# One chain for both directions' triangular inverses in the DeltaNet part of an encoder layer, with projections moved beside it

## The chip, the cores and the metric

The kernel runs on one core of a Trainium2 chip. The metric is the device time of one execution in microseconds. A core has five instruction streams that run side by side and meet through semaphores: TensorE (PE, matmuls; its weight loads are counted as PEld), VectorE (DVE), ScalarE (ACT), GpSimd (POOL) and SyncE (SP), which here does nothing but issue DMAs. Each stream executes its instructions in the order of the program.

## The reference, cut to what matters

Two layers of a hybrid encoder, on 512 tokens with 1024 features. Each layer normalises its input and projects it for three mixers: windowed attention (6 query heads on 2 key heads), a bidirectional gated DeltaNet (6 heads) and a bidirectional RWKV-7 (4 heads). Their outputs are concatenated, projected by one matrix and added to the residual; then comes a gated MLP.

```python
def layer(h, l):
    u = rms_norm(h, norm_mix[l])
    qa, ka, va, dn_qkv, dn_z, dn_a, dn_b, rw_in = split(u @ w_in[l])
    ya = banded_window_attention(rope(qa), rope(ka), va, sink[l])
    ys = gated_delta(dn_qkv, dn_a, dn_b) + reversed(gated_delta(reversed ...))
    yd = rms_norm(ys, dn_norm[l]) * silu(dn_z)
    yr = rwkv7(rw_in)
    h = h + concat([ya, yd, yr]) @ w_out[l]
    return h + gated_mlp(rms_norm(h, norm_ffn[l]))
```

Inside the DeltaNet, tokens go in 8 chunks of 64 per head. Each chunk needs the inverse of a unit lower triangular 64x64 matrix:

```python
lower = where(strict, (k_beta @ k.T) * decay, 0)
a_mat = lower + eye(C)
sol = triangular_solve(a_mat, rhs, lower=True, unit_diagonal=True)
```

With 6 heads, 8 chunks and two directions these are 96 matrices per layer.

## The kernel before

Features lie on the partitions and the 512 tokens along the free axis, so a tile of 128 features is 128x512. Float32 products are made in three matmuls: each operand is split in a high and a low part, and `product` (L313) issues high x high (L319), low x high (L320) and high x low (L321) for each k-tile of 128. A weight tile therefore passes three engines: SP loads `wr` (L305), ACT rounds it to `wh` (L308), POOL subtracts to give `wl` (L309). There are three buffers of each. A 128-column projection of the layer's input (`proj`) is 8 k-tiles, 24 matmuls of 512 columns, from two weight tiles of 128x512.

PSUM tiles come from four streams: "j" (2 buffers) for projections, "r" (3) for RWKV and attention, "d" (2) for DeltaNet, "o" (1). A projection's result stays in its "j" buffer until DVE has read it.

`layer` (L868) emits, in this order: RWKV preparation, its inverse and its scan over 8 chunks (`rwkv_scan`), with the attention projections handed in at steps 2 to 6 (K, V and the three query tiles q0, q1, q2); DeltaNet preparation (`dn_prep`) for two more head pairs; the RWKV output `rwkv_out`; the DeltaNet inverse; `finish_inverse`; the DeltaNet scan (`dn_scan`), with the gates z0, z1 and z2; `dn_out`; the output projection; the MLP. A scheduler then puts each engine's instructions in an order by its own reckoning, so an instruction can stand well ahead of where it is written.

The inverse of a 64x64 matrix is made of two 32x32 inverses and a product. `invert` (L378) does the 32x32 blocks by elimination: the blocks' rows lie on the 128 partitions (four groups of 32) and 32 problems lie along the free axis. A 32x32 transpose (L383 or L385) turns them so that each partition holds one whole problem of 32x32; then for j = 1 to 30 one instruction multiplies (L390) and one adds (L391), on r x j elements with r = 31 - j; then two transposes (L397, L398) bring it back. The forward direction's elimination runs on DVE, the backward one's on POOL, each with 60 instructions. What goes in are the negated diagonal blocks, copied by ACT in 24 instructions on 32 partitions (L984). `finish_inverse` (L401) then makes the product for the off-diagonal block with small matmuls (L411, L417), and ACT copies the parts into place (L413, L421, L425).

An attention block (`attn_head`, L830; there are 12 per layer, 3 query tiles x 4 token blocks) makes scores by matmul (L842), masks them and takes the maximum on DVE (L843), exponentials on ACT (L852), divides on DVE (L856), transposes on PE (L859) and multiplies by the values (L863). Five of them are written beside the inverse, seven in the DeltaNet scan. `rope` (L821) scales a projection on DVE (L823), rotates it by a matmul (L825), multiplies by the sine on DVE (L826) and by the cosine on POOL (L827) and adds on DVE (L828). `gate_proj` (L928) multiplies the projection by the normalisation on DVE (L931), makes a sigmoid on ACT (L932) and multiplies on DVE (L933). L695 and L696 in `dn_prep` scale keys and queries by their inverse norms, which a matmul (L693) and ACT (L346) make. In the scan of the DeltaNet, L773 is the matmul on the state and L778 the subtraction that follows on DVE. `split` (L249) makes a mixer output's high part on ACT (L253) and its low part on DVE (L254). The output projection takes 8 k-tiles for each of 8 output tiles j, 24 matmuls each.

Times below are of the second layer.

Of the kernel before, what the change touches and what calls it, by code (L numbers as in the profile page):

```python
# [14 lines left out]
P = 128  # L15
T = 512
# [20 lines left out]
def _const_array():  # L37
    """Everything here depends on shapes alone."""
# [19 lines left out]
    for name, v in (("eps", EPS), ("rweps", RW_EPS), ("one", 1.0), ("halfpi", math.pi / 2)):  # L58
        add(name, np.full((P, 1), v))
    add("ident", np.eye(P))  # L60
# [29 lines left out]
# per-feature parameters, as columns of 128 values  # L90
# [6 lines left out]
def _param_array(inputs):  # L97
    """[128, layer, column]: the parameters as they are, laid out by feature."""
# [15 lines left out]
def trunk(tc, t, out):  # L114
# [14 lines left out]
    # Slots of a tag are handed out in program order, so each stream of work has its own.  # L129
# [6 lines left out]
    def p4(*free, dt=F32):  # L136
        return bp.tile([P, *free], dt, tag="p4", bufs=20, name=nm("p4"))
# [12 lines left out]
    def sm(*free):  # L150
        return bp.tile([P, *free], F32, tag="sm", bufs=7, name=nm("sm"))

    def tiny(*free, tag="tiny"):
        return bp.tile([P, *free], F32, tag=tag, bufs=1 if len(free) > 1 else 3, name=nm(tag))

# [1 line left out]
    cst = cp.tile([P, _CONST.shape[1]], F32, name="cst")  # L157
    par = cp.tile([P, DEPTH, NPAR], F32, name="par")
# [31 lines left out]
    sinkb = [cp.tile([P, 6], F32, name=nm("sink")) for _ in range(DEPTH)]  # L190
# [7 lines left out]
    def derive_params():  # L198
        for l in range(DEPTH):
            pt = par[l]  # L200
            pc = lambda name, n: pt[:, at[name] : at[name] + n]
            dv = cp.tile([P, 24], F32, name=nm("dv"))
            # 0:8 centre weight of the token shift, 8:10 -k_k, 10:12 1-k_a, 12:16 -w0, 16:20 -a0
# [18 lines left out]
    cos_t = cp.tile([P, T], F32, name="cos_t")  # L222
    sin_t = cp.tile([P, T], F32, name="sin_t")
# [36 lines left out]
    class Norm:  # L260
        """Collects x tiles as they are finished: squares summed, x*g split in two parts."""
# [86 lines left out]
    def chunk_sums(dst, src, backward):  # L348
        """running sums over the tokens of each chunk"""
# [6 lines left out]
    def tok_major(st, src, evac):  # L356
        """[128 (h d), 512 tokens] -> [(h, token), chunk, d]; evac(dst slice maker, psum piece)"""
# [11 lines left out]
    def run(g):  # L369
        """the value a generator returns"""  # L370
# [7 lines left out]
    def invert(dpk, upper, E, work):  # L378
        """dpk [128, 32, 32]: strictly triangular 32x32 blocks N (row on the partition, problem, column).
        Returns (I-N)^-1 as it lies and transposed, in the same form; E does the elimination."""  # L380
# [19 lines left out]

    def finish_inverse(st, o1, o2, units, upper, sign):  # L401
        """units: (problem, matrix tile, chunk): fills tile[:, chunk, 0:64] with (I-N)^-1."""
# [52 lines left out]
        # normalised key  # L455
# [9 lines left out]
        # bonus  # L465
# [645 lines left out]
```

## Time and profile before

| | us |
|---|---|
| three timed runs | 1732.46, 1734.43, 1734.72 (median 1734.43) |
| span of the profiled execution | 1732.2 |
| RWKV scan from its third step, DeltaNet preparation, RWKV output | 1104 to 1176 |
| both 32x32 inverses | 1176 to 1222 |
| rest of the inverse | 1222 to 1247 |
| DeltaNet scan | 1247 to 1309 |
| DeltaNet output and output projection | 1309 to 1359 |

The profile is one execution on the chip. A group of instructions is given by its line in the program, engine and operation, what it writes and reads, count, busy time, the mean of one in ns, and the idle time just before them on their engine with what ended it. PEclk is the clock that was granted to TensorE in a stretch: 1.00 is 2.4 GHz, 0.50 is 1.2 GHz, and values between are a mix of the two. A matmul's own length in a timeline includes its way through the array; successive ones start closer together than they are long. The rows on which the prediction rests stand in their own section below.

### The profile page before, as it was taken

Reading aid. Unit: us, or ns where it says so; the run is one execution under the profiler, and the core shown is the slowest. Engines: PE = TensorE matmul, PEld = TensorE weight load, DVE = VectorE, ACT = ScalarE, POOL = GpSimd, SP = SyncE. Lnnn points to the kernel's source line nnn. Section 1 sums busy time; section 2 is a strip of 40 time slices with the busy share of each in tenths; the row PEclk is TensorE's granted clock in tenths of the full one; section 3 lists DMA queues with packets and bytes.
Section 4 is the critical chain, followed back from the end, with each engine's and each line's share of the span. In section 5 each row is a group of like instructions: output and inputs, shape, how many; then the busy total and the mean of one; then the engine's idle time right before and its main releaser. Section 6 shows DMA issues by size and latency. Waiting matters only on the chain. (4 is left out here: it accounts for less than half of the span.)

```text
span 1732.2 us, 29160 instructions
## 1 busy us (share of the span) xinstructions
PE 1537.9 (89%) x11500; PEld 1204.0 (70%) x11500; DVE 952.5 (55%) x1583; ACT 821.4 (47%) x1541; POOL 704.9 (41%) x632
## 2 busy tenths in 40 slices
PE   7988789359999999999998897982799999999997
PEld 4676666247678888888876676651577788888885
DVE  6478945775535555531136797578563455555001
ACT  5556453446445444443335754362744544444321
POOL 4321323431165555545543122426013655555553
PEclk9989979658999999999999998995799999999998
DMA  5311211100043333333342012220002333333332
GB/s 166 79 39 50 63 48 44 37 1 15 26 128 92 97 97 98 97 104 113 114 104 74 20 50 50 59 66 1 2 21 80 110 98 98 97 97 97 93 99 91
DMA packets 230537, 126.07 MB, mean 73 GB/s; under 512 B 23656, under 2 KB 221416, under 8 KB 230400
## 3 DMA queue, kind: packets, MB, share of 16 engines
q1 hardware_dynamic: 228624, 121.02, 25.0%
q10 hardware_dynamic: 1776, 3.20, 0.6%
q8 instruction: 90, 1.47, 0.4%
q14 instruction: 47, 0.39, 0.1%
HBM read 117.84 MB, written 6.34 MB: 72 GB/s over the span
## 5 line engine op out<-in xcount | busy, mean ns | idle before, releaser
L309 POOL TENSOR_TENSOR wl<-wr,wh 128x512 fp32r<-128x512 f32 (+1 forms) x408 | 555.9, 1365 | 760.9 <-ACT wh L308 714.5
L319 PE MATMUL ps<-hh,wh 128*128 128x512 f32 x1248 | 502.7, 403 | 21.2 <-ACT wh L308 18.6
L320 PE MATMUL ps<-hl,wh 128*128 128x512 f32 x1248 | 502.1, 402 | 0.0
L321 PE MATMUL ps<-hh,wl 128*128 128x512 f32 x1248 | 498.7, 400 | 0.4 <-POOL wl L309 0.4
L308 ACT ACTIVATE wh<-wr 128x512 fp32r<-128x512 f32 (+1 forms) x408 | 250.8, 618 | 444.5 <-PE ps L320 393.4
L319 PEld LDWEIGHTS ps<-hh,wh 128*128 128x128 f32 x1248 | 236.4, 190 | 80.2 <-ACT wh L308 19.5
L320 PEld LDWEIGHTS ps<-hl,wh 128*128 128x128 f32 x1248 | 236.3, 189 | 55.8 <-issue 3.7
L321 PEld LDWEIGHTS ps<-hh,wl 128*128 128x128 f32 x1248 | 235.8, 189 | 55.6 <-issue 3.9
L1063 DVE TENSOR_TENSOR p<-ps,p 128x512 f32<-128x512 f32 x16 | 11.1, 692 | 198.8 <-PE ps L321 198.8
L859 PE MATMUL ps<-cst,cv 128*128 128x128 f32 x120 | 24.9, 341 | 85.0 <-DVE cv L856 84.5
L320 PE MATMUL ps<-p,wh 128*128 128x512 f32 x256 | 99.6, 389 | 0.0
L319 PE MATMUL ps<-p,wh 128*128 128x512 f32 x256 | 99.6, 389 | 0.0
L321 PE MATMUL ps<-p,wl 128*128 128x512 f32 x256 | 99.6, 389 | 0.0
L1040 DVE TENSOR_TENSOR tr<-ps,rb 128x512 f32<-128x512 f32 x44 | 30.4, 692 | 100.3 <-PE ps L321 100.3
L859 PEld LDWEIGHTS ps<-cst,cv 128*128 128x128 f32 x120 | 15.7, 168 | 95.5 <-issue 67.4
L747 POOL TENSOR_TENSOR sm<-sm,gl 128x384 f32<-128x384 f32 x12 | 10.8, 903 | 129.9 <-DVE sm L776 72.8
L1043 DVE SCALAR_TENSOR_TENSOR td<-tr,par,td 128x511 f32<-128x511 f32 x44 | 39.1, 889 | 34.9 <-ACT td L1042 34.9
L1043 DVE SCALAR_TENSOR_TENSOR tr<-td,par,tr 128x511 f32<-128x511 f32 x44 | 36.5, 830 | 35.0 <-ACT tr L1042 35.0
L319 PEld LDWEIGHTS ps<-p,wh 128*128 128x128 f32 x256 | 48.1, 188 | 10.0
L321 PEld LDWEIGHTS ps<-p,wl 128*128 128x128 f32 x256 | 48.1, 188 | 9.9
L320 PEld LDWEIGHTS ps<-p,wh 128*128 128x128 f32 x256 | 48.1, 188 | 9.9
L279 POOL TENSOR_TENSOR tr<-tr,tr 128x512 f32<-128x512 f32 x32 | 42.8, 1337 | 28.0 <-issue 8.7
(292 smaller groups left out, 2597.6 us busy)
## 6 DMA issues: line engine op xcount, KB each, us to landing
wr<-ffn_w_up SPq DMA_DIRECT2D x176, 256.0 KB, 2.9
wr<-w_in SPq DMA_DIRECT2D x88, 256.0 KB, 2.8
wr<-ffn_w_down SPq DMA_DIRECT2D x80, 256.0 KB, 2.8
wr<-w_in SPq DMA_DIRECT2D x24, 128.0 KB, 2.4
p<-scr ACTq DMA_DIRECT2D x12, 256.0 KB, 3.6
wr<-w_out SPq DMA_DIRECT2D x32, 96.0 KB, 2.6
wr<-w_out SPq DMA_DIRECT2D x16, 192.0 KB, 3.0
p<-xt SPq DMA_DIRECT2D x8, 256.0 KB, 3.7
```

Source lines behind the costliest of these rows:

```text
L279: G.tensor_tensor(acc, self.acc, sq, add)
L308: S.activation(hi[:, :n, :], raw[:, :n, :], AF.Copy)
L309: G.tensor_tensor(lo[:, :n, :], raw[:, :n, :], hi[:, :n, :].bitcast(F32), sub)
L319: PE.matmul(o, wh, xh, start=k == 0, stop=False)
L320: PE.matmul(o, wh, xl, start=False, stop=False)
L321: PE.matmul(o, wl, xh, start=False, stop=k == n - 1)
L747: G.tensor_tensor(gs, state, flat(gl, step), mult)
L859: PE.transpose(pp[:, P * j : P * j + P], scs[g][:, P * j : P * j + P], ident)
L1040: V.tensor_tensor(u, o, nf.rb, mult)
L1043: V.scalar_tensor_tensor(a[:, 1:], u[:, :-1], w(0), a[:, 1:], mult, add)
L1063: V.tensor_tensor(x1[j], o, x1[j], add)
```

## The change

1. The two directions' eliminations become one chain on DVE (`invert_both`) over a persistent tile `pair_sq` of 128 x 2 x 32 x 32: 60 instructions on 2 x r x j elements (L432, L433). POOL no longer eliminates.
2. The negated diagonal blocks are made by six DVE instructions on 128x256 (`neg_diag32`, L418 and L420) in place of the 24 copies of ACT.
3. K and V stay in the RWKV scan. The query projections and the gates are written as a `fill` beside the inverse, one for every second elimination step. Behind them stand eight `rwkv_share(j)`: RWKV's two k-tiles of the output projection, 6 matmuls from a weight tile of 128x256; the result is added to the residual tile (L1039) and written to DRAM (`xr`, L1040).
4. The output projection takes 6 k-tiles instead of 8 for each j, 18 matmuls, and adds `xr` (L1093) in place of the residual.
5. Two of the twelve attention blocks are written behind the inverse and ten in the DeltaNet scan (two at each of the first three steps).
6. The pool of 128x1024 tiles has 24 buffers for 20; small constants, parameters and tables share one tile `fixed`.

By the scheduled order, q0's and z0's products still stand in the RWKV scan; q1, z1, q2, z2 and the shares stand beside the inverse. The order is the same in both programs up to the third step of the RWKV scan and from the MLP on.

```diff
+    def neg_diag32(dst, mt, upper):
+        lo, hi, m = mt[:, :, 0:32], mt[:, :, 32:64], C("m32")
+        if upper:
+            V.scalar_tensor_tensor(dst, hi, m[:, 1:2], lo, mult, sub)
+        else:
+            V.scalar_tensor_tensor(dst, lo, m[:, 0:1], hi, mult, sub)
+
+    def invert_both(dpks, work):
+        L = pair_sq
+        for d in range(2):
+            a = L[:, d]
+            V.transpose(a.rearrange("p s t -> p t s") if d else a, dpks[d].rearrange("q p t -> q t p"))
+        yield
+        for j in range(1, 31):
+            r = 31 - j
+            tmp = work[:, : 2 * r * j].rearrange("p (d r j) -> p d r j", d=2, j=j)
+            V.tensor_tensor(tmp, L[:, :, j + 1 : 32, j : j + 1].broadcast_to([P, 2, r, j]), L[:, :, j : j + 1, 0:j].broadcast_to([P, 2, r, j]), mult)
+            V.tensor_tensor(L[:, :, j + 1 : 32, 0:j], L[:, :, j + 1 : 32, 0:j], tmp, add)
+            yield
+        G.memset(L.rearrange("p d a b -> p d (a b)")[:, :, 0:1024:33], 1.0)
...
@@ layer
-            if i >= 2:
-                heads += [next(ap, None)]
-        k, vt, *qs = heads[:5]
+            if i in (2, 4):
+                heads += [next(ap)]
+        k, vt = heads
...
+        yh, yl = p4(2, T, dt=F32R), p4(2, T, dt=F32R)
+        for pr_, y in enumerate(yr):
+            S.activation(yh[:, pr_, :], y, AF.Copy)
+            V.tensor_tensor(yl[:, pr_, :], y, yh[:, pr_, :].bitcast(F32), sub)
+        rw_parts = [(yh[:, pr_, :], yl[:, pr_, :]) for pr_ in range(2)]
+        wo = t["w_out"][l]
+        wr = wo[768:1024].rearrange("(k p) m -> p k m", p=P)
+        xr = dp.tile([P, KT, T], F32, name=nm("xr"))
+
+        def rwkv_share(j):
+            xo = t2("r")
+            nc.sync.dma_start(xo, xd[:, j, :])
+            o = ps("j")
+            product(o, weights(lambda raw, k0, k1: [(raw, wr[:, k0:k1, P * j : P * j + P])], 2), rw_parts)
+            V.tensor_tensor(xo, o, xo, add)
+            nc.sync.dma_start(xr[:, j, :], xo)
+
+        def fill():
+            for i in range(3):
+                qs.append(next(ap))
+                yield
+                gate_proj(i, zss[i])
+                yield
+            for j in range(KT):
+                rwkv_share(j)
+                yield
...
             for p in range(NPAIR_DN):
-                for h in range(0, P, 32):
-                    S.activation(dpk[h : h + 32, 8 * p : 8 * p + 8, :], dn["rm"][p][d][h : h + 32, :, h % 64 : h % 64 + 32], AF.Copy, scale=-1.0)
+                neg_diag32(dpk[:, 8 * p : 8 * p + 8, :], dn["rm"][p][d][:, :, 0:64], d == 0)
             dpks.append(dpk)
-        work = cv()
-        fw, bw = invert(dpks[0], True, V, work[:, :256]), invert(dpks[1], False, G, work[:, 256:])
+        both_ways, filler = invert_both(dpks, cv()), fill()
         for i in range(31):
-            next(bw)
-            next(fw)
-            if i % 6 == 5:
-                next(att, None)
-        inv = [run(fw), run(bw)]
+            next(both_ways)
+            if i % 2 == 1:
+                next(filler, None)
+        inv = run(both_ways)
+        for _ in range(2):
+            next(att)
...
-        gate_proj(0, zss[0])
         dn["o"] = [p4(2, T), p4(2, T)]
         for i, _ in enumerate(dn_scan(dn)):
-            if i < 2:
-                gate_proj(1 + i, zss[1 + i])
             next(att, None)
+            if i < 3:
+                next(att, None)
...
-        mixed = [split(y, None, "h", i) for i, y in enumerate(yt + yr + yd)]
+        mixed = [split(y, None, "h", i) for i, y in enumerate(yt + yd)]
...
-            nc.sync.dma_start(xo, xd[:, j, :])
+            nc.sync.dma_start(xo, xr[:, j, :])
             o = ps("j")
-            product(o, weights(pieces, KT), mixed)
+            product(o, weights(pieces, 6), mixed)
```

The order on DVE at the start of the inverse, in the first layer, before. `p_2919` is the forward direction's tile, `cv_2916` the products; L843 to L856 are an attention block:

```order
L385 STREAM_TRANSPOSE p_2917<-p_2902 128x32x32
L383 STREAM_TRANSPOSE p_2919<-p_2888 128x1024
L843 ISA cv_2942,mx_2944<-ps_2945,cst,sink_86 128x256
L843 ISA mx_2944 128x1
L390 TENSOR_TENSOR cv_2916<-p_2919 128x30
L843 ISA cv_2943,mx_2944<-ps_2948,cst,sink_86 128x256
L843 ISA mx_2944 128x1
L391 TENSOR_TENSOR p_2919<-p_2919,cv_2916 128x30
L847 TENSOR_TENSOR es_2952<-sink_86,mx_2944 128x2
L848 TENSOR_SCALAR nmx_2951<-mx_2944 128x2
L390 TENSOR_TENSOR cv_2916<-p_2919 128x58
L391 TENSOR_TENSOR p_2919<-p_2919,cv_2916 128x29x2
```

The same place after. `at_` and `tr_` are the query ropes, `p_2735` is the gate z1, which DVE takes from PSUM `ps_2810`:

```order
L427 STREAM_TRANSPOSE pair_sq<-p_2749 128x32x32
L872 TENSOR_TENSOR at_2798<-at_2798,tr_2799 128x512
L432 TENSOR_TENSOR cv_2754<-pair_sq 128x60
L975 TENSOR_TENSOR p_2735<-ps_2810,rb_88 128x512
L433 TENSOR_TENSOR pair_sq<-pair_sq,cv_2754 128x2x30
L867 SCALAR_TENSOR_TENSOR tr_2897<-ps_2857,rb_88 128x512
L432 TENSOR_TENSOR cv_2754<-pair_sq 128x116
L433 TENSOR_TENSOR pair_sq<-pair_sq,cv_2754 128x2x29x2
L432 TENSOR_TENSOR cv_2754<-pair_sq 128x168
L433 TENSOR_TENSOR pair_sq<-pair_sq,cv_2754 128x2x28x3
L432 TENSOR_TENSOR cv_2754<-pair_sq 128x216
L977 TENSOR_TENSOR p_2735<-p_2735,tr_2847 128x512
```

The elimination had attention blocks between its steps; now its steps share DVE's order with the ropes (L867, L870, L872) and gates (L975, L977), and L975 and L867 read projections from PSUM.

The DMA issues on SP at the same place, before. `wr` are weight tiles, here those of the output projection:

```order
L619 DMA tr_2850<-aside_157 128x512
L620 DMA tr_2851<-aside_157 128x512
L305 DMA wr_3719<-w_in 128x4x128
L305 DMA wr_4529<-w_out 64x3x128 x2
L619 DMA tr_2868<-aside_157 128x512
L620 DMA tr_2869<-aside_157 128x512
L305 DMA wr_4529<-w_out 128x128
L305 DMA wr_4537<-w_out 128x128
```

And after. `xr_2743` is the new tile in DRAM; the weight tiles of 128x2x128 are those of the shares:

```order
L318 DMA wr_3161<-w_out 128x2x128
L1036 DMA tr_3053<-xt 128x512
L1036 DMA tr_3074<-xt 128x512
L1036 DMA tr_3095<-xt 128x512
L1036 DMA tr_3116<-xt 128x512
L1036 DMA tr_3137<-xt 128x512
L1040 DMA xr_2743<-tr_3053 128x512
L1036 DMA tr_3158<-xt 128x512
L318 DMA wr_3182<-w_out 128x2x128
L1040 DMA xr_2743<-tr_3074 128x512
L1036 DMA tr_3179<-xt 128x512
L318 DMA wr_3203<-w_out 128x2x128
```

The loads of the output projection's weights and residual have moved behind the shares' loads and, from L1040 on, between writes that each wait for a sum on DVE.

## Rows read from the trace of the kernel before

**Rows 1.** Page: span, busy time of PE, and one group of DVE.

```profile
span 1732.2 us, 29160 instructions
...
PE 1537.9 (89%) x11500; PEld 1204.0 (70%) x11500; DVE 952.5 (55%) x1583; ACT 821.4 (47%) x1541; POOL 704.9 (41%) x632
...
L1040 DVE TENSOR_TENSOR tr<-ps,rb 128x512 f32<-128x512 f32 x44 | 30.4, 692 | 100.3 <-PE ps L321 100.3
```

**Rows 2.** Windows: stretch, length, busy PE, PEld, DVE, ACT, POOL, clock, DMA share, GB/s.

```profile
1104.00:1176.00 72.00, 57.65 (x692) 39.22 (x690) 43.59 (x71) 39.10 (x84) 22.46 (x27) 0.93 0.21 60
1176.00:1222.00 46.00, 16.64 (x60) 9.73 (x60) 42.24 (x102) 8.06 (x27) 31.76 (x62) 0.54 0.00 1
1222.00:1247.00 25.00, 19.55 (x410) 14.52 (x412) 11.90 (x23) 19.94 (x51) 0.00 (x0) 0.69 0.01 2
1247.00:1309.00 62.00, 58.89 (x1074) 46.58 (x1067) 38.53 (x123) 31.65 (x87) 8.38 (x8) 1.00 0.05 15
1309.00:1361.00 52.00, 48.48 (x201) 36.80 (x199) 20.02 (x27) 26.78 (x45) 30.19 (x23) 1.00 0.39 112
```

**Rows 3.** Timeline of PE, half clock then full: start, length, line.

```profile
1084.31 0.63 PE L320 MATMUL ps<-hl,wh 128*128 128x512 f32 x1
1084.73 0.63 PE L321 MATMUL ps<-hh,wl 128*128 128x512 f32 x1
...
1329.76 0.39 PE L320 MATMUL ps<-hl,wh 128*128 128x512 f32 x1
...
1331.12 0.39 PE L320 MATMUL ps<-hl,wh 128*128 128x512 f32 x1
```

**Rows 4.** Groups by line of DVE from 1104 to 1176.

```profile
L828 DVE TENSOR_TENSOR at<-at,tr 128x512 f32<-128x512 f32 x4 | 4.0, 993 | 1.8 <-POOL tr L827 1.8
...
L826 DVE TENSOR_TENSOR at<-ps,sin_t 128x512 f32<-128x512 f32 x4 | 2.8, 688 | 1.7 <-PE ps L825 1.7
...
L593 DVE TENSOR_TENSOR sm<-ps,sm 128x256 f32<-128x256 f32 x5 | 2.1, 425 | 4.5 <-PE ps L590 4.5
L823 DVE SCALAR_TENSOR_TENSOR tr<-ps,rb 128x512 f32<-128x512 f32 x3 | 2.0, 683 | 0.0
```

**Rows 5.** Waits of DVE, 1140 to 1176: us in total, times, longest.

```profile
DVE p L385 <- ACT p L984: 8.1, 1, 8.1
DVE cv L695 <- ACT td L346: 4.2, 1, 4.2
DVE cv L696 <- ACT td L346: 2.2, 1, 2.2
```

**Rows 6.** Groups by line of ACT from 1164 to 1176.

```profile
L984 ACT ACTIVATE p<-p 32x256 f32<-32x256 f32 x24 | 9.9, 414 | 0.3
```

**Rows 7.** Groups by form of DVE from 1015 to 1068, RWKV's inverse.

```profile
L383 DVE STREAM_TRANSPOSE p<-p 128x1024 f32<-128x1024 f32 x1 | 2.0, 1958 | 0.0
...
L390 DVE TENSOR_TENSOR tr<-p 128x240 f32<-128x240 f32 x2 | 0.8, 400 | 0.0
...
L390 DVE TENSOR_TENSOR tr<-p 128x30 f32<-128x30 f32 x2 | 0.4, 198 | 0.1
```

**Rows 8.** Groups by form of DVE from 1176 to 1220, the DeltaNet inverse.

```profile
L390 DVE TENSOR_TENSOR cv<-p 128x238 f32<-128x238 f32 x2 | 1.3, 667 | 0.1
```

**Rows 9.** Timeline of DVE and POOL in RWKV's inverse.

```profile
1039.27 1.48 DVE L391 TENSOR_TENSOR p<-p,tr 128x240 f32<-128x240 f32 x1
...
1039.22 1.26 POOL L309 TENSOR_TENSOR wl<-wr,wh 128x512 fp32r<-128x512 f32 x1 [7.59 <-ACT wh L308]
```

**Rows 10.** Groups by line of DVE from 1247 to 1309, the DeltaNet scan.

```profile
L843 DVE CUSTOM_DVE_ANT_0 cv<-ps,cst,sink 128x384 f32<-128x384 f32 (+1 forms) x12 | 6.1, 548 | 0.4 <-PE ps L842 0.4
...
L856 DVE TENSOR_SCALAR cv<-cv,den 128x384 f32<-128x384 f32 (+1 forms) x14 | 4.8, 389 | 0.2
...
L778 DVE TENSOR_TENSOR sm<-ps,sm 128x384 f32<-128x384 f32 x6 | 3.3, 558 | 12.3 <-PE ps L773 12.3
```

**Rows 11.** Timeline of DVE, the last DeltaNet part's split.

```profile
1320.94 0.69 DVE L254 TENSOR_TENSOR hl<-p,hh 128x512 fp32r<-128x512 f32 x1 [0.70 <-ACT hh L253]
```

More of the change, by code (lines that the diff above doesn't have):

```diff
@@ L59, in _const_array @@
         add(name, np.full((P, 1), v))
+    hi32 = (i % 64 >= 32).astype(np.float32)
+    add("m32", np.stack([hi32 - 1.0, -hi32], 1))
     add("ident", np.eye(P))
@@ L136, in p4 @@
     def p4(*free, dt=F32):
-        return bp.tile([P, *free], dt, tag="p4", bufs=20, name=nm("p4"))
+        return bp.tile([P, *free], dt, tag="p4", bufs=24, name=nm("p4"))
     def t2(stream, *free, dt=F32):
@@ L150, in sm @@
     def sm(*free):
-        return bp.tile([P, *free], F32, tag="sm", bufs=7, name=nm("sm"))
+        n = math.prod(free)
+        a = bp.tile([P, T], F32, tag="sm", bufs=7, name=nm("sm"))[:, :n]
+        return a.rearrange("p (a b) -> p a b", b=free[1])
+    small_at = {}
     def tiny(*free, tag="tiny"):
+        if len(free) > 1:
+            lo = W + DEPTH * NPAR + 2 * T + 48 * small_at.setdefault(tag, len(small_at))
+            names = " ".join("abc"[: len(free)])
+            return fixed[:, lo : lo + math.prod(free)].rearrange(f"p ({names}) -> p {names}", **dict(zip("abc", free)))
         return bp.tile([P, *free], F32, tag=tag, bufs=1 if len(free) > 1 else 3, name=nm(tag))
-    cst = cp.tile([P, _CONST.shape[1]], F32, name="cst")
-    par = cp.tile([P, DEPTH, NPAR], F32, name="par")
+    W = _CONST.shape[1]
+    fixed = cp.tile([P, W + DEPTH * NPAR + 2 * T + 384], F32, name="fixed")
+    cst = fixed[:, :W]
+    par = fixed[:, W : W + DEPTH * NPAR].rearrange("p (l n) -> p l n", l=DEPTH)
     n0, n1 = CONSTS["ident"][0], PARAM_AT["dn_conv"]
@@ L189, in trunk @@
     cols, abias, acoef = [], [], []
-    sinkb = [cp.tile([P, 6], F32, name=nm("sink")) for _ in range(DEPTH)]
+    sinkb = [fixed[:, W + DEPTH * NPAR + 2 * T + 288 + 6 * l :][:, :6] for l in range(DEPTH)]
     def late_params():
@@ L201, in derive_params @@
             pc = lambda name, n: pt[:, at[name] : at[name] + n]
-            dv = cp.tile([P, 24], F32, name=nm("dv"))
+            dv = fixed[:, W + DEPTH * NPAR + 2 * T + 240 + 24 * l :][:, :24]
             V.tensor_tensor(dv[:, 0:8], pt[:, at["rw_mu"] : at["rw_mu"] + 8], pt[:, at["rw_mu"] + 8 : at["rw_mu"] + 16], add)
@@ L219, in trunk @@
     exp_ln_tables()
-    cos_t = cp.tile([P, T], F32, name="cos_t")
-    sin_t = cp.tile([P, T], F32, name="sin_t")
+    pair_sq = cp.tile([P, 2, 32, 32], F32, name="pair_sq")
+    cos_t, sin_t = fixed[:, W + DEPTH * NPAR : W + DEPTH * NPAR + T], fixed[:, W + DEPTH * NPAR + T : W + DEPTH * NPAR + 2 * T]
     def rotary_tables():
@@ L399, in invert @@
         return o1, o2
+    def neg_diag32(dst, mt, upper):
[17 more added lines that the diff above has]
+        G.memset(L.rearrange("p d a b -> p d (a b)")[:, :, 0:1024:33], 1.0)
+        res = []
+        for d in range(2):
+            o1, o2 = p4(32, 32), p4(32, 32)
+            nat, swp = L[:, d], L[:, d].rearrange("p a b -> p b a")
+            V.transpose(o1.rearrange("q p c -> q c p"), swp if d else nat)
+            V.transpose(o2.rearrange("q p c -> q c p"), nat if d else swp)
+            res.append((o1, o2))
+        return res
     def finish_inverse(st, o1, o2, units, upper, sign):
@@ L836, in attn_head @@
             m0 = P * (k0 - nb + 1)
-            scs = [cv(384), cv(384)]
+            scs = [cv(), cv()]
             mxt = tiny(2, tag="mx")
@@ L888, in layer @@
                 nc.sync.dma_start(wau[64:128], t["rw_a_up"][l].rearrange("d r c -> r d c"))
-                gup = bp.tile([P, 256], F32, tag="gup", name=nm("gup"))
+                gup = bp.tile([P, T], F32, tag="gup", name=nm("gup"))[:, :256]
                 nc.sync.dma_start(gup, t["rw_g_up"][l])
@@ L973, in layer @@
         yr = [rwkv_out(l, rw, pr_, None) for pr_ in range(2)]
-        pa, pb, pc_ = p4(2, T), p4(2, T), None
+        pa, pb, pc_ = p4(2, T), p4(2, T), p4(2, T)
         yt = [pa[:, 0, :], pa[:, 1, :], pb[:, 0, :]]
-        zss = [pb[:, 1, :]]
+        zss = [pb[:, 1, :], pc_[:, 0, :], pc_[:, 1, :]]
         att = attention()
+        qs = []
+        yh, yl = p4(2, T, dt=F32R), p4(2, T, dt=F32R)
[22 more added lines that the diff above has]
+                yield
         dpks = []
```

7 lines of the change are left out of this document (2 added, 5 removed).

## The prediction

> **What bounds the kernel now.** The page's head comes first [rows 1]: PE is busy for 89% of the span, so most of the 1732.2 us is matmuls in a row, and what leaves PE's list or fills a hole in it counts. The order of the two programs differs only between the third step of the RWKV scan and the end of the output projection, in layer 1 from 1104 to 1361 us. The table of stages [rows 2] is read next. From 1104 to 1176 (RWKV scan, DeltaNet preparation, RWKV output) PE is busy 57.65 of 72 us and DVE 43.59; here PE is late. From 1176 to 1222 (the inverse) DVE is busy 42.24 of 46 us, POOL 31.76, PE 16.64 at a granted clock of 0.54: DVE is the bound and PE has a hole of some 30 us. Then come ACT's stage (1222 to 1247: ACT 19.94 of 25), the DeltaNet scan (PE 58.89 of 62) and the output projection (PE 48.48 of 52). The first layer goes through the same stages, so I work in layer 1 and double.
>
> **The change part by part, per layer.** A 512-column product costs the matmuls' pitch: at full clock six of them lie between 1329.76 and 1331.12, 0.227 us each; at the half clock it is 1084.73 - 1084.31 = 0.42 [rows 3].
>
> *RWKV scan and preparation, 72.2 us.* Of 120 such products 48 stay (q0, z0); q1, q2 and z1 leave. That is 72 x 0.227 = 16.3 us less for PE, whose 57.65 falls to about 41, level with DVE. What DVE gains in time: the ropes of q1 and q2, 2 x (0.683 + 0.688 + 0.993) = 4.7 us, and about half of the waits beside them (1.8 and 1.7), 1.7 [rows 4]. DVE waits 4.2 and 2.2 us at L695 and L696 [rows 5] for a normalisation whose matmul stands behind those products on PE: 6.4, gone. Last, L385 waits 8.1 us [rows 5] for 24 ACT copies of 0.414 us (9.9) [rows 6]; six DVE instructions on 128x256 take their place. The nearest row is L593's, 128x256 with two operands, at 0.425 [rows 4]; 6 x 0.425 = 2.5 are added, and two subtractions for the share's second part, 2 x 0.69 = 1.4 [rows 11]. The scan's waits on PE, 4.5 at L593 [rows 4], fall by about another 1.0. Sum: -4.7 -1.7 -6.4 -8.1 +2.5 +1.4 -1.0 = **-18**. If L695's wait is a chain and no queue, and the scan's waits stay, it is about -10; if all of L593's go and as much again at the lines beside it, -23.
>
> *Inverse, 46.0 us.* Before, DVE has 30 pairs of instructions of r x j elements and POOL has as many; after, DVE has 30 pairs of 2rj. Without POOL beside it such an instruction took 198 ns for 30 elements and 400 for 240 [rows 7]: 169 + 0.962 per element. The sum of rj over j = 1 to 30 is 4960, so the 60 take 2 x (30 x 169 + 0.962 x 9920) = 29.2 us, with 0.035 of gap each 31.3; a 480-element one is beyond the rows and read off the line. Two transposes at 1.96 [rows 7] add 3.9. So the chain itself is 35 us: less than the 42 of before, because POOL's own elimination had made DVE's slower (667 ns for 238 elements, where 400 had done [rows 8]).
> The work beside it goes through DVE as well, and in DVE's order: three gates at 2 x 0.69 (4.1), the last of q0's rope (0.7, the size of L826), the ropes of q1 and q2 (4.7), eight sums of the shares at 0.692 (5.5, priced as L1040 [rows 1]) and the DVE side of two attention blocks, 4.7. Sum 54.7.
> POOL now splits weights here: about 5 of 128x512 and 9 of 128x256, and two rope products, some 15 us. The nearest row: an elimination instruction of 240 elements, 0.40 alone, took 1.48 beside one L309 of 1.26 on POOL, a loss of 1.08 [rows 9]. Seven long ones by 1.08 and nine short by about half would be 12; not each meets a two-input instruction from SBUF, and I take 10. Below, none, if POOL's fall into instructions that read PSUM: L1040, one operand from PSUM, kept 0.692 on the average of 44 in the feed-forward part, where POOL splits weights all along. Above, POOL's whole 15.
> DVE also waits in order on PE now: L975 (gate), L867 (rope) and L1039 (share) each stand between elimination instructions; if the product is late, the elimination behind it stands still. PE needs 144 x 0.227 = 32.7 us plus two attention blocks, well under the stage, so I count 2. Total 67: **+21**, bounds +11 and +30.
> The Trainium skill (SBUF — State Buffer, Who interferes with whom) says that a DVE instruction with two SBUF inputs contends with a GpSimd instruction that reads SBUF, and that the one that comes second is blocked for the other's whole length. The 1.08 of 1.26 agrees for one pair; applied to every POOL instruction it gives the 15 instead of the 10, which is the rival "whole hold" below.
> ACT's wh copies and sigmoids (ACT is busy 8.06 of 46) are hidden by DVE. SP's reads of x and writes of the shares stand between weight loads, and each write waits for a sum on DVE, with the loads of the next weights behind it. The loads run two or more ahead, so nothing; if that lead is gone, some 2 us a load, inside the range.
>
> *Finish of the inverse, 25 us.* Bound by ACT's small copies, of the form of those in [rows 6]; ACT is busy 19.94 of 25 [rows 2]. Its attention part moves away, transposes are now four in a row: **-3**, between -5 and 0.
>
> *DeltaNet scan, 62 us.* Ten attention blocks instead of seven, gate's work gone. A block has on DVE 2 x 0.548 and 2 x 0.389 [rows 10] plus small ones, in all some 2.4. 3 x 2.4 = 7.2, less the four gate instructions of 0.69 there (2.8), is 4.4. PE's share is hidden only in part: DVE waits 12.3 us at L778 for PE [rows 10], which says that PE's own chain sets the step, and z2's 24 products (5.4) leave it as the blocks' matmuls come. I take +4, and +1 for the last block's chain: **+5**, between +1 and +8.
>
> *Output, 49.5 us.* 48 products fewer are 10.9 us. The last DeltaNet part is split at 1320.94 [rows 11]; until then only products of the finished parts can fill PE, now 18 instead of 30 per two tiles. That gives back about 2: **-9**, between -11 and -5. Reading xr instead of x costs the same transfer.
>
> Sum: -18 + 21 - 3 + 5 - 9 = -4 a layer, -8 in all. The profiled execution's 1732.2 us lie 2.2 under the median of the runs, 1734.43; the same offset gives 1724.2 + 2.2 = **1726 us**.
>
> **The rivals.**
> *Light POOL.* The POOL holds and the waits on PE hardly bite, and the inverse is 57: -14 a layer, -28, about **1706**. For it: the chain's 35 us is simple arithmetic, and a DVE reading PSUM kept its time beside POOL. Against: half of DVE's added work has two SBUF inputs.
> *Whole hold.* Every POOL instruction costs DVE its whole length: +5, net +1 a layer, about **1736**.
> *The slower side: PE stays at the half clock in the inverse.* Its products now come in groups of 24 and 6, each after weights or an evacuation that DVE's order delays. The stage stood at 0.54 with PE busy 16.64 of 46 [rows 2], and the finish stage at 0.69 though PE was busy 19.55 of 25: being busy for most of a stage did not bring the clock up. At 0.42 instead of 0.22 the 144 products take 62 us, and with the blocks' matmuls of some 7 and the elimination waiting in DVE's order about 77 are needed: +10, net +6 a layer, about **1746**. It decides if the granted clock of this stage reads under about 0.75.
> *RWKV scan a chain.* If L695's and the scan's waits stay, that stage gives only 10: net +4 a layer, about **1742**.
>
> **How the numbers follow.** A measurement of this kernel can tell about 0.2%, 3.5 us, from no change. The forecast of 1726 has 0.42, with an own range of 1718 to 1734 (0.35 of it under 1731, 0.07 within 3.5 us); light POOL 0.22, whole hold 0.12 (0.09 within, 0.03 slower), half clock 0.16, scan a chain 0.08. Faster 0.57, same 0.16, slower 0.27. Both signs have weight, since the net is a difference of -30 and +26. The range runs from 1704, a little under light POOL, to 1745, just short of the half clock's full price; about 0.1 lies below and 0.1 above.
>
> **What would show it.** In the profile of after: the inverse stage (from the first L427 to the last L433) at 60 to 72 us with 60 elimination instructions summing to 30 us plus what POOL holds; DVE's waits on L975, L867 and L1039 summing to under 5; no wait on a copy ahead of L427; the stretch from the RWKV scan to L427 some 18 shorter; the output projection at 40 us; the granted clock of the inverse above 0.75. The forecast is wrong if the inverse lies beyond 57 to 76, if the clock stays low, or if the stretch ahead of it shrinks by under 10.

## The result, and the profile after

The changed kernel took 1740.09 us (median of 8 runs) against 1732.78 us (8 runs of the kernel before): a ratio of 1.0051, 95% interval 1.0034 to 1.0068. It is slower; 1726 was forecast, and a gain was given the larger chance. The profiled execution of after (span 1747.0 us, 14.8 above that of before) is the slowest of its eight, whose times go with the clock granted to TensorE over the whole span (1736.0 us at 0.935, 1748.8 at 0.922), so up to 4 us a layer of the growth below belong to this execution and not to the median.

Windows of the second layer after, with the columns of [rows 2]: RWKV scan and preparation, inverse, its finish, DeltaNet scan, output.

```profile
1112.50:1165.80 53.30, 42.47 (x640) 31.12 (x638) 41.32 (x74) 28.80 (x60) 17.45 (x22) 0.95 0.18 46
1165.80:1225.00 59.20, 42.74 (x149) 30.28 (x149) 56.06 (x104) 15.09 (x36) 19.05 (x17) 0.79 0.36 113
1225.00:1246.50 21.50, 16.04 (x404) 13.28 (x402) 8.70 (x10) 18.22 (x44) 0.00 (x0) 0.50 0.01 2
1246.50:1325.70 79.20, 71.77 (x1089) 54.68 (x1088) 39.73 (x147) 31.02 (x95) 5.13 (x6) 0.92 0.02 5
1325.70:1380.00 54.30, 46.74 (x168) 33.17 (x167) 23.83 (x28) 26.57 (x48) 29.35 (x25) 0.91 0.35 105
```

Cut at the same events in both kernels (from the third step of the RWKV scan; then first transpose of the inverse, first transpose back, first matmul of the DeltaNet scan, last sum of the scan, first evacuation of the MLP), the mean of the two layers is:

| stage | before, us | after, us | change | forecast |
|---|---|---|---|---|
| RWKV scan, preparation | 71.9 | 53.4 | -18.4 | -18 |
| inverse | 45.8 | 60.8 | +14.9 | +21 |
| finish | 25.9 | 21.4 | -4.5 | -3 |
| DeltaNet scan | 63.2 | 80.8 | **+17.6** | +5 |
| output | 55.8 | 53.9 | **-1.9** | -9 |

Three stages came out as worked out or better. The scan took all of it back, and the output projection gave little.

The inverse first. The two groups of the elimination, on DVE, in the second layer (line, count, busy us, mean ns, idle):

```profile
L433 DVE TENSOR_TENSOR pair_sq<-pair_sq,cv 128x60 f32<-128x60 f32 (+14 forms) x30 | 18.7, 623 | 0.5
L432 DVE TENSOR_TENSOR cv<-pair_sq 128x60 f32<-128x60 f32 (+14 forms) x30 | 17.3, 577 | 0.5
```

Together 36.0 us, where the straight line through [rows 7] gave 29.2. The largest step lies near that line when nothing holds it (480 elements: 0.658 us, 0.631 by the line). Of the other 6.8 us, 6.2 are in the 16 instructions that overlap one of POOL's; POOL is busy 19.05. So POOL costs the elimination about a third of POOL's time here, not its whole length. The waits on PE in DVE's order, of which 2 us were forecast, sum there to 2.0 us (1.0 at L1039, 1.0 at L887) and in the first layer to 3.7.

The scan is told by PE's score matmuls (L842 before, L886 after) and the last products of a block (L863, L907). In the scan before, start and length:

```profile
1273.61 0.83 PE L863 MATMUL ps<-tr,at 128*64 128x128 f32 x8
1275.44 0.70 PE L842 MATMUL ps<-at,at 64*128 64x256 f32 x4
1281.24 0.65 PE L863 MATMUL ps<-tr,at 128*64 128x128 f32 x4
1282.79 0.65 PE L863 MATMUL ps<-tr,at 128*64 128x128 f32 x4
1283.86 0.92 PE L842 MATMUL ps<-at,at 64*128 64x384 f32 x4
1289.82 1.14 PE L863 MATMUL ps<-tr,at 128*64 128x128 f32 x12
1291.73 0.92 PE L842 MATMUL ps<-at,at 64*128 64x384 f32 x4
```

And after:

```profile
1270.44 0.65 PE L907 MATMUL ps<-tr,at 128*64 128x128 f32 x4
1271.39 0.91 PE L886 MATMUL ps<-at,at 64*128 64x384 f32 x2
1272.22 0.65 PE L907 MATMUL ps<-tr,at 128*64 128x128 f32 x4
1272.81 0.91 PE L886 MATMUL ps<-at,at 64*128 64x384 f32 x2
1278.53 1.20 PE L907 MATMUL ps<-tr,at 128*64 128x128 f32 x12
1279.66 0.92 PE L886 MATMUL ps<-at,at 64*128 64x384 f32 x4
1286.85 1.19 PE L907 MATMUL ps<-tr,at 128*64 128x128 f32 x12
1287.97 0.70 PE L886 MATMUL ps<-at,at 64*128 64x256 f32 x4
```

In both, one block's scores start as the last one's product ends or soon after, 8 us apart (1283.86 to 1291.73 before, 1271.39 to 1279.66 to 1287.97 after). After, that holds for the whole scan: the scores of nine blocks start from 1254.20 to 1318.1, 8.0 us apart on average. Ten blocks at 8 us are 80, and the scan of after is 80.8. Before, one block stands in each step of the scan, its scores 0.8 to 1.3 us ahead of the step's matmuls on the state (L750), so the same rows don't tell whether the blocks or the state set the pitch there.

### The profile page after: what moved, and what is told of

It is laid out like the page before. It is cut to its first block, busy times and chain, and to the rows that moved or that the text cites. A ratio compares the mean times of both kernels' runs of the same rounds, so it can differ in the third digit from the quotient of the medians.

```text
span 1747.0 us, 29033 instructions
## 1 busy us (share of the span) xinstructions
PE 1564.1 (90%) x11500; PEld 1226.6 (70%) x11500; DVE 1021.4 (58%) x1611; ACT 786.2 (45%) x1509; POOL 653.7 (37%) x526
## 5 line engine op out<-in xcount | busy, mean ns | idle before, releaser
L332 PE MATMUL ps<-hh,wh 128*128 128x512 f32 x1216 | 491.4, 405 | 18.7 <-ACT wh L321 17.8
L333 PE MATMUL ps<-hl,wh 128*128 128x512 f32 x1216 | 491.7, 405 | 8.6 <-DVE hl L270 4.4
L334 PE MATMUL ps<-hh,wl 128*128 128x512 f32 x1216 | 484.8, 399 | 0.4 <-POOL wl L322 0.4
L332 PE MATMUL ps<-p,wh 128*128 128x512 f32 x288 | 114.0, 396 | 7.0 <-ACT wh L321 4.2
L334 PE MATMUL ps<-p,wl 128*128 128x512 f32 x288 | 113.7, 395 | 0.3 <-POOL wl L322 0.3
L333 PE MATMUL ps<-p,wh 128*128 128x512 f32 x288 | 113.5, 394 | 0.0
L332 PEld LDWEIGHTS ps<-p,wh 128*128 128x128 f32 x288 | 54.7, 190 | 20.9 <-ACT wh L321 5.4
L791 POOL TENSOR_TENSOR sm<-sm,fixed 128x384 f32<-128x384 f32 x12 | 10.3, 855 | 157.4 <-DVE sm L822 79.7
L1109 DVE TENSOR_TENSOR tr<-ps,rb 128x512 f32<-128x512 f32 x44 | 30.4, 692 | 59.4 <-PE ps L334 59.4
L333 PEld LDWEIGHTS ps<-p,wh 128*128 128x128 f32 x288 | 54.8, 190 | 11.2
L887 DVE CUSTOM_DVE_ANT_0 cv<-ps,fixed 128x256 f32<-128x256 f32 (+1 forms) x48 | 25.3, 549 | 61.3 <-PE ps L886 61.3
L1112 DVE SCALAR_TENSOR_TENSOR td<-tr,fixed,td 128x511 f32<-128x511 f32 x44 | 40.0, 909 | 36.1 <-ACT td L1111 36.1
L1113 DVE SCALAR_TENSOR_TENSOR tr<-td,fixed,tr 128x511 f32<-128x511 f32 x44 | 56.9, 1292 | 1.6
L1115 ACT ACTIVATE tr<-tr 128x512 f32<-128x512 f32 x44 | 27.8, 633 | 61.5 <-DVE tr L1113 61.4
L1112 DVE SCALAR_TENSOR_TENSOR tr<-td,fixed,tr 128x511 f32<-128x511 f32 x44 | 33.8, 768 | 35.0 <-ACT tr L1111 35.0
```

The lines of the kernel that those rows point to most:

```text
L332: PE.matmul(o, wh, xh, start=k == 0, stop=False)
L333: PE.matmul(o, wh, xl, start=False, stop=False)
L334: PE.matmul(o, wl, xh, start=False, stop=k == n - 1)
L887: V.tensor_tensor_reduce(scs[g][:, :W], pss[:, :W], C("attm")[:, m0 : m0 + W], 1.0, sinkb[l][:, tq + 3 * g : tq + 3 * g + 1], add, mx, mxt ...
L1109: V.tensor_tensor(u, o, nf.rb, mult)
L1112: V.scalar_tensor_tensor(a[:, 1:], u[:, :-1], w(0), a[:, 1:], mult, add)
```

## Experiments

Each ratio is to the kernel before, timed on the same chip. Scan and other stages are means of the two layers, cut as in the table above.

**Five blocks beside the inverse again.** The attention blocks alone are put back.

```diff
             if i % 2 == 1:
                 next(filler, None)
+            if i % 6 == 5:
+                next(att)
         inv = run(both_ways)
-        for _ in range(2):
-            next(att)
...
             next(att, None)
-            if i < 3:
-                next(att, None)
```

> The changed kernel with five attention blocks written beside the inverse and seven in the DeltaNet scan, as before; all else as changed. Theory 'blocks': each attention block in the scan costs about 3 us, because its maximum and its division stand on VectorE ahead of the state's own instructions; three fewer shorten the scan from about 80 to about 71 us in each layer and lengthen the inverse by 3 x 2.4 = 7 us; net -2 a layer, about 1736 us in all. Theory 'clock': the scan is long because TensorE enters it at the half clock; then the scan falls by under 4 us, the inverse grows by 7, and the time is about 1747 us.

Measured 1720.27 us, ratio 0.9908 (0.9889 to 0.9927). Its inverse, finish and scan in the second layer:

```profile
1148.30:1213.40 65.10, 47.91 (x197) 32.55 (x197) 59.84 (x122) 19.25 (x50) 16.91 (x16) 0.83 0.26 81
1213.40:1238.40 25.00, 17.55 (x416) 13.14 (x414) 12.39 (x23) 21.72 (x54) 1.27 (x1) 0.73 0.18 59
1238.40:1297.80 59.40, 57.39 (x1032) 46.27 (x1032) 33.20 (x116) 23.42 (x71) 5.04 (x6) 0.94 0.03 7
```

The scan falls by 21.4 us, not 9; inverse and finish together grow by 7.8. That is 7 us for each of three blocks in the scan, with what the clock does in it (0.94 here, 0.87 and 0.92 in after), and 2.6 for each outside it. The direction of "blocks" was right; its reason (a block's VectorE work ahead of the state's) gives less than half.

**The gate z2 in the finish.** Its 24 products are tied there through their PSUM stream.

```diff
-        o = proj(l, parts, COL_Z + P * pr_)
+        o = proj(l, parts, COL_Z + P * pr_, st=st)
...
+        late = (2,)
...
             finish_inverse("d", *inv[d], [(8 * p + c, dn["rm"][p][d], c) for p in range(3) for c in range(NCH)], d == 0, -1.0)
+            if d == 0:
+                for i in late:
+                    gate_proj(i, zss[i], "d")
```

> The changed kernel with the products of the gate z2 (24 matmuls) taken from the inverse and tied to the finish of the inverse, between the two directions; all else as changed. Theory 'clock': these products bring the granted clock up before the scan starts; the clock of the scan reads above 0.95 instead of 0.87 to 0.92, its first step falls by 4 us, the scan to about 75 us, finish +1, inverse -2: -5 a layer, about 1730 us. Theory 'blocks': the scan stays within 2 us of 80, and the time within 4 us of 1740.

Measured 1742.82 us, ratio 1.0041 (1.0024 to 1.0057): no difference from the changed kernel. Finish and scan of the second layer:

```profile
1218.50:1245.70 27.20, 21.19 (x431) 17.27 (x432) 10.87 (x17) 23.05 (x56) 1.97 (x2) 0.75 0.06 17
1245.70:1317.60 71.90, 63.28 (x1070) 49.18 (x1066) 38.19 (x137) 28.30 (x87) 5.65 (x6) 0.98 0.02 6
```

The clock of the scan did rise to 0.98 and the scan fell to 71.9, but one block had moved ahead of it as well, and the finish paid 6 us. The run doesn't separate the clock from the moved block, and the clock is not had for nothing.

**No shares.** The output projection takes its eight k-tiles and the residual again.

```diff
-            for j in range(KT):
-                rwkv_share(j)
-                yield
...
-            product(o, weights(pieces, 6), mixed)
+            product(o, weights(pieces, KT), mixed)
```

> The changed kernel without the shares of RWKV beside the inverse: the output projection takes its eight k-tiles and the residual again, as before. Theory 'filler': the shares took away the matmuls that filled TensorE while the DeltaNet output was made, so the output stage grows by only about 3 us when they come back, and the inverse loses 8 sums of 0.69 and the waits and POOL work beside them, about 8 us: -5 a layer, about 1730 us. Rival, as forecast: 48 products cost 9 us in the output stage and the inverse gives back 6: +3 a layer, about 1746 us.

Measured 1732.00 us, ratio 0.9976 (0.9963 to 0.9988). The output stage grows by 2.8 us for 48 products that alone take 10.9, as "filler" had it; the inverse gives back 2.0 us and not 8, the stretch ahead of it 5.5. Its scan, with the same ten blocks, is 75.4 us at a clock of 0.96, 5.4 shorter than in after (0.92 in the second layer, 0.87 in the first). Cut at the second group of matmuls on the state (L794), after's scan and then this one's are, in the second layer:

```profile
1246.50:1265.10 18.60, 16.50 (x185) 12.48 (x184) 6.35 (x22) 7.73 (x22) 1.26 (x2) 0.68 0.01 2
1265.10:1325.70 60.60, 55.27 (x906) 42.20 (x904) 33.38 (x125) 23.29 (x73) 3.87 (x5) 0.99 0.02 6
```

```profile
1231.20:1245.90 14.70, 14.05 (x185) 10.73 (x184) 6.37 (x22) 5.99 (x17) 0.84 (x1) 0.79 0.01 2
1245.90:1306.50 60.60, 54.94 (x904) 41.72 (x904) 33.37 (x125) 23.34 (x73) 4.19 (x5) 1.00 0.02 6
```

The whole difference lies in the first part, where the clocks differ (in the first layer 21.9 us at 0.53 against 14.7 at 0.79). The half clock covers 13.2 and 20.7 us of after's two scans and 6.1 of each here. Where PE sets the pace, a stretch at the half clock does half the work of one at the full clock, and half of the excess, 3.6 and 7.3 us, is close to the 3.9 and 7.2 by which the first parts differ, so the clock accounts for the 5.4; no run changes the clock alone.

**All three edits.**

> All three of these edits together: five blocks beside the inverse, z2 in the finish, no shares; one chain on VectorE, the VectorE negation and the queries and gates z0, z1 beside the inverse stay. If the three causes add up: per layer 53.5 before the inverse, 59 inverse, 22 finish, 67 scan, 57 output, 258.5 in place of 270: about 1718 us. If they do not add (the same TensorE time is only moved about), about 1730 us.

Measured 1723.28 us, ratio 0.9924 (0.9907 to 0.9941): between the two expectations. Six blocks are left in the scan, which takes 55.6, but the finish takes 35.7 us with the blocks and z2 in it.

**Five blocks, no shares.** The first and the third edit together.

> The changed kernel with five attention blocks beside the inverse (as in e1_blocks5) and without RWKV's shares (as in e3_no_share); z2 stays beside the inverse. If the share's price seen in e3_no_share (6 us a layer) is its own and not that of the clock in the scan, the time falls from the 1720 of e1_blocks5 to about 1708 us. If most of those 6 us were the scan's clock, which five blocks beside the inverse already cure, it stays at 1716 to 1722 us.

Measured 1722.13 us, ratio 0.9916 (0.9897 to 0.9935): the second case, at its upper edge. Without shares the stretch up to the inverse is 6 us shorter, but the finish goes to 29.9 us at a clock of 0.50, where it takes 25.0 at 0.73 with the shares just ahead of it:

```profile
1209.90:1239.80 29.90, 25.68 (x422) 17.86 (x422) 11.38 (x22) 21.80 (x55) 0.00 (x0) 0.50 0.01 2
```

**Eight blocks, and all twelve, ahead of the scan.** One block at every fourth step of the elimination, or at every second.

```diff
+            if i >= 4 and i % 4 == 0 and done < 8:
+                next(att)
+                done += 1
```

> The changed kernel with eight attention blocks written beside the inverse and four in the scan; shares stay. Theory 'five us a block in the scan, two to two and a half outside it', read from scans of 55.6, 59.4, 71.9 and 75.4 us with 6, 7, 9 and 10 blocks: three fewer than in e1_blocks5 take the scan from 59.4 to about 46 us and add 7 before it: -6 to -8 a layer, about 1706 us. Rival 'the state's chain is the floor': a step without a block still takes 6.5 us, the scan stays above 52, and the time is about 1722 us.

> The changed kernel with all twelve attention blocks written ahead of the finish of the inverse; the scheduler may still let a few slip into the first steps of the scan. A measure of the scan's steps without a block. By 5 us a block the later steps take about 4.5 us each and the scan about 45; the ten blocks cost some 22 us ahead of it, so the time is about 1722 us. By the rival a step without a block takes 6.5 us, the scan stays above 52 and the time goes to 1736 us or more.

Measured 1731.05 us (0.9977, 0.9961 to 0.9993) and 1736.38 us (0.9996, 0.9977 to 1.0014). The scan of the first falls only to 55.7, that of the second to 53.0. Three blocks still end in the first steps of the second one's scan; the steps behind them, without a block, take 5.2 to 5.7 us, not 6.5 and not 4.5. From e1_blocks5 to e6_blocks8 the rest of the layer grows by 9.2 us for three blocks, some 3 each. My 5 us a block was a straight line through points of a curve with a bend: with three, four and six blocks the scan takes 53.0, 55.7 and 55.6 us, with seven 59.4, and with ten 75.4 to 80.8. That below the bend the state's own chain sets the length fits these runs.

**The negation alone, in the kernel before.** `neg_diag32` in place of the 24 copies.

> The kernel before with one part of the change alone: the negated diagonal blocks by six VectorE instructions in place of ScalarE's 24 copies. VectorE's wait of 8.1 us ahead of the inverse goes and 2.5 us of work come: -5.6 a layer, -11 us in all. Rival: the wait only changes its name (another engine is as late there), and the time stays within 3 us of the kernel before.

Measured 1723.67 us, ratio 0.9929 (0.9910 to 0.9948). The stretch up to the inverse falls by 5.9 us a layer. This one part is worth 12 us, most of what any variant here gained: the 0.9908 of e1_blocks5 can't be told from it, the 0.9890 of e13_best just can.

**One block a step.** Two are left over and are written behind the scan.

```diff
             next(att, None)
-            if i < 3:
-                next(att, None)
```

> The changed kernel with the same two attention blocks ahead of the scan, but only one written at each of its eight steps; the two that are left are written behind the scan. Theory 'backlog': a block that is written steps ahead of where it runs stands in front of the state's own instructions on VectorE and TensorE, and makes a step 9.5 to 10.5 us with one or one and a half blocks in it, where a block that lags makes it 7.4; with one a step the scan's middle steps fall to about 7.5, the two blocks behind cost about 6, and scan and output together fall by about 12 us a layer: about 1718 us. Theory 'count': ten blocks cost what ten cost, wherever written; the time stays within 5 us of 1740.

Measured 1745.51 us, ratio 1.0066 (1.0040 to 1.0092). The scan falls to 62.3, and the output stage grows from 53.9 to 73.1. PE there, behind the scan:

```profile
1312.02 0.92 PE L886 MATMUL ps<-at,at 64*128 64x384 f32 x4
1312.86 1.12 PE L856 MATMUL ps<-td,fixed 128*128 128x512 f32 x2
1319.29 1.54 PE L903 MATMUL ps<-fixed,cv 128*128 128x128 f32 x6 [5.31 <-DVE cv L900]
1320.77 2.18 PE L907 MATMUL ps<-tr,at 128*64 128x128 f32 x12
1322.88 1.23 PE L886 MATMUL ps<-at,at 64*128 64x256 f32 x4
1327.44 1.08 PE L903 MATMUL ps<-fixed,cv 128*128 128x128 f32 x4 [3.33 <-DVE cv L900]
```

"Backlog" falls as an account of the whole: the three blocks that end behind the scan cost 19 us there, 6 each, with PE waiting for DVE inside (5.31 and 3.33 us in the rows). So a block in a chain is dear behind the scan too; beside the inverse it cost 2.6 us (e1_blocks5).

**Four blocks.** Beside the inverse, and one a step.

> The changed kernel with four attention blocks beside the inverse and one at each of the eight steps of the scan. By the prices so far (a lagging block about 2 us in the scan, 3 ahead of it) it is 0 to 1 us a layer shorter than e1_blocks5: about 1719 us. If a block in the scan costs 5 us whatever its place, it is 2 us a layer longer: about 1725 us.

Measured 1723.05 us, ratio 0.9938 (0.9914 to 0.9961). It doesn't tell the two apart.

**Seven blocks, written early.** The blocks of the first experiment, with two at each of the first three steps.

> e1_blocks5 with one edit: its seven blocks in the scan are written two at each of the first three steps and one at the fourth, so they run ahead of the steps; the number in the scan is the same. Theory 'backlog': the first four or five steps take 9.5 to 11 us in place of 6.1 to 8.9, the last ones 5.5; the scan grows from 59.4 to 66 or more, +6 a layer, about 1733 us. Theory 'count': the scan stays within 2 us of 59.4 and the time within 4 us of 1720.

Measured 1730.68 us, ratio 0.9987 (0.9971 to 1.0004). The scan takes 64.3 against 59.4: with the blocks done early the last steps run bare. The place counts for 5 us; the other 16 to after's scan are the number and the clock together.

**More room in PSUM.** By now the chain of blocks was seen. Each block needs four PSUM tiles of stream "r", of whose three slots one is held by the output of the whole head. The edit gives the transposes the two slots of "j", idle in the scan.

```diff
+    pp_stream = ["r"]
...
-                pp = ps("r")
+                pp = ps(pp_stream[0])
...
+        pp_stream[0] = "j"
         for i, _ in enumerate(dn_scan(dn)):
```

> The changed kernel with one edit: the attention blocks in the scan put their transposes into the two PSUM slots of stream j, which is idle there, in place of the two free slots of stream r. Theory 'chain of blocks, made by PSUM': the next block's scores no longer wait for the last one's product, the pitch of the blocks falls from 8 us to 6.5 or less while there is a backlog, the scan from about 80 to about 67, the time to about 1716 us. Theory 'the blocks' own work': PE and VectorE have no room for a second block in a step; the pitch stays at 7.5 or more, the scan above 75 and the time above 1732 us.

Measured **1717.98 us, ratio 0.9894 (0.9878 to 0.9910)**. Nothing else of the change was touched, and ten blocks still end in the scan, though three of them, not one, now have their scores in the finish, which grows by 2.1 us. Its scan, and PE in it (scores are L888, products L909):

```profile
1226.80:1292.50 65.70, 62.39 (x1074) 50.01 (x1074) 39.17 (x139) 29.21 (x92) 5.04 (x6) 0.94 0.02 6
```

```profile
1248.54 1.15 PE L909 MATMUL ps<-tr,at 128*64 128x128 f32 x12
1250.46 0.91 PE L888 MATMUL ps<-at,at 64*128 64x384 f32 x4
1251.79 0.70 PE L888 MATMUL ps<-at,at 64*128 64x256 f32 x2
1255.16 0.88 PE L905 MATMUL ps<-fixed,cv 128*128 128x128 f32 x6
1256.35 1.20 PE L909 MATMUL ps<-tr,at 128*64 128x128 f32 x12
1257.48 0.66 PE L905 MATMUL ps<-fixed,cv 128*128 128x128 f32 x4
1258.44 0.87 PE L909 MATMUL ps<-tr,at 128*64 128x128 f32 x8
1260.09 0.70 PE L888 MATMUL ps<-at,at 64*128 64x256 f32 x4
1267.16 0.92 PE L888 MATMUL ps<-at,at 64*128 64x384 f32 x4
1275.02 0.92 PE L888 MATMUL ps<-at,at 64*128 64x384 f32 x4
1282.94 0.70 PE L888 MATMUL ps<-at,at 64*128 64x256 f32 x4
```

At 1251.79 the next block's scores run while the block before still waits for its transposes (1255.16), and the two blocks' last products end within 1.8 us of each other (1257.55 and 1259.31). The scan falls from 80.8 to 65.1, and from e3_no_share's 75.4, at about the same clock, by 10.3. So the chain that kept the backlog of blocks from overlapping was made by the two free slots. From 1260.09 on, with the backlog gone and one block in each step, the blocks still follow each other at 7.1 to 7.9 us: that pitch is not the slots'.

The Trainium skill (Perfetto Trace Analysis, Optimization Strategy) says that a gap that repeats on an engine that should be full can mean that SBUF or PSUM has no room for the next tile. The sign doesn't show here: in after PE has no idle stretch above 0.72 us between 1260 and 1320, and what repeats is the blocks' pitch of 8 us. The cause does: the run with two slots more shows that PSUM was short.

**Both.** That edit on the kernel with five blocks beside the inverse.

> e1_blocks5 (five blocks beside the inverse, seven in the scan, one a step) with the transposes of the scan's blocks in stream j. Seven blocks at 8 us are 56 of its scan of 59.4, so by 'chain of blocks, made by PSUM' the scan falls to the 55 seen with four to six blocks, about -4 a layer, and the time to about 1712 us. By the rival it stays within 4 us of 1720 us.

Measured 1717.05 us, ratio 0.9890 (0.9874 to 0.9905): the shortest of all, by less than can be told from e12_more_psum, and within the 4 us of the rival. The scan falls from 59.4 to 57.9, not to 55:

```profile
1234.90:1292.90 58.00, 56.17 (x1023) 45.92 (x1022) 32.80 (x109) 22.94 (x71) 5.03 (x6) 0.92 0.03 7
```

With seven blocks, one a step, the slots are worth 1.6 us of the scan. That their chain filled the scan of seven blocks isn't borne out.

## Why the prediction failed

**The scan (+5 forecast, +17.6) is the step that failed.** It priced a block at its DVE busy time, "in all some 2.4" us, and took three of them less the gates' work. A block is scores on PE, maximum on DVE, exponentials on ACT, division on DVE, transposes on PE, copy on ACT, product on PE, one after another; its length was 8 us, and the next could not begin ahead of its end. The forecast had read from [rows 10] that PE's chain sets the step, and still priced the blocks on DVE; the trace of before showed that each step already holds one block, end to end with the next. What it costs when two blocks must share a step, that trace could not show. By differences between runs, the scan's growth is: three blocks, 16 (e1_blocks5 to after is 21.4, of which e3_no_share puts 5.4 beside the lower clock); the clock, 5.4 in this profile, which the forecast put at nothing; the rest, with the gates gone, -3.8 (e1_blocks5 against before, both with seven). That they add up to 17.6 follows from how they are taken.

**The clock was thought of in the wrong place.** The rival "half clock" put it into the inverse, with a bound of 0.75; the inverse read 0.79 and 0.77 and was set by DVE (56.06 of 59.20 us busy), so this rival did not come about, though its 1746 and its sign were near. The half clock is in the finish and at the scan's entry. Before, 24 products of a gate ran there from 1234.63 to 1258; this is a stretch of 3 us just behind their start, of before and then of after (where the finish begins 2.8 us later):

```profile
1237.00:1240.00 3.00, 3.00 (x83) 2.39 (x83) 0.00 (x0) 2.43 (x7) 0.00 (x0) 0.94 0.02 5
```

```profile
1237.00:1240.00 3.00, 2.36 (x88) 2.22 (x82) 0.69 (x4) 2.90 (x8) 0.00 (x0) 0.50 0.02 5
```

Before, the clock is at 1.00 from 1240 on; after, it still reads 0.50 from 1249 to 1252, with the scan begun. In the first layer before's scan too begins at the half clock, for 6.6 us, after's for 20.7. The forecast took those 24 products off the scan as a gain of 5.4 us and didn't ask what they did for the clock.

**The output (-9 forecast, -1.9).** The forecast gave back 2 us for lost filler. 48 products are 10.9 us, but PE's busy time falls by 6.1 only (the mean of the two layers; its clock reads 0.94 and 0.91, before 1.00 in both), and its idle time grows by 4.2. This is the second layer before, with PE's longest wait between the DeltaNet parts, and then the two longest after, one for ACT and one for DVE:

```profile
1309.20:1364.80 55.60, 51.78 (x215) 39.20 (x214) 20.61 (x26) 28.15 (x48) 32.11 (x24) 1.00 0.39 112
1318.97 0.73 PE L319 MATMUL ps<-hh,wh 128*128 128x512 f32 x2 [1.16 <-ACT hh L253]
```

```profile
1331.10 1.81 PE L856 MATMUL ps<-td,fixed 128*128 128x512 f32 x2 [1.30 <-ACT td L854]
1338.02 0.63 PE L333 MATMUL ps<-hl,wh 128*128 128x512 f32 x1 [2.05 <-DVE hl L267]
```

After, the products between these parts run in part at the half clock up to 1341 (0.66 and 0.82 in two successive stretches of 5 us). e3_no_share confirms the size: 2.8 us.

**What held.** The stretch up to the inverse: -18.4 for -18, with L695's and L696's waits gone, and the negation's -5.9 a layer for the -5.6 of its terms, shown alone by e7_before_neg. The inverse: 36.0 us of elimination for 39 (29.2 and 10 of hold) and DVE's other work as priced; it lies inside its bounds, nearer the light end, so "whole hold" did not come about: the hold on the elimination was 6.8 us where 10 were taken. "RWKV scan a chain" did not either.

The range's upper end, 1745, holds 1740; the sign and the likeliest case were wrong, since one term of the sum was mis-sized by 13 us a layer and another by 7, and the inverse, 6 us better than forecast, hid part of it. None of the three signs given for a wrong forecast came about (inverse 60.8, clock 0.77 and 0.79, the stretch ahead shorter by 18.4): all three looked at the part that held, none at the scan.

Two lengths in the prediction, 72.2 and 49.5 us, are not those of the rows (72.0, and 50 in the table of stages), and 144 products at 0.42 us are 60.5, not 62. No term of the sum changes by that. L773 and L778 of [rows 10] make the new state, and L778 is an addition, not a subtraction; the matmul on the state is L750.

## What to carry to other kernels

Work that is moved into a stage as "filler" is priced by the length of its own chain and by how many copies of it can be open at once, not by its busy time on the bound engine. Look in the trace for the pitch at which such pieces follow each other: where each begins as the last one ends, one more piece can cost its whole length, and whether it does is a question for a run. Then look for what ties them; here it was two slots of PSUM. Freeing two more took the kernel from 1.0051 to 0.9894 of before's time; moving three pieces out of the stage took it to 0.9908, which the intervals don't tell apart, and both together to 0.9890.

## What the runs showed of the hardware

A stage of small matmuls did not bring TensorE's clock up though it was busy: the finish reads 0.50 with PE busy 25.68 of 29.90 us in e5_blocks5_no_share. In e1_blocks5 the same stage reads 0.73 and takes 25.0 us: the clock, full while the last shares' 512-column products run, stays so until 1218.3 and is full again from 1228.5 to 1235.3, behind six more such products and a block's matmuls (in e5_blocks5_no_share the same six lie between 1213.83 and 1233.73, and it stays at 0.50). The shares ahead of the stage are not enough for it: in after their last product starts at 1214.62, 10 us before the finish, which reads 0.50 throughout. So products that are moved away can cost elsewhere what their place gains: without the shares the kernel takes 1722.13 us, with them 1720.27.

An elementwise instruction of DVE on 480 elements in one chain takes 0.658 us where two of 240 take 0.400 each [rows 7]: joining two directions on one engine saves 0.14 us there, and 0.16 at 60 elements (0.234 against two of 30 at 0.198 each). Sixty times that is about 9 us a layer against two chains on the same engine, an estimate; no run has both chains on DVE apart.
